# Seven-product projections on one core: accumulators as single PSUM banks, sums on VectorE, x read again for its sums, the attention's loads in a new order

## The chip, the core and the metric

The kernel runs on one core of a Trainium2 chip. The metric is device time in microseconds (us) of one execution. The engines are TensorE (PE in the profile; PEld are its weight loads), VectorE (DVE), ScalarE (ACT), GpSimd (POOL) and SyncE (SP, which here only issues DMAs). Each engine works through its own instructions in order.

## The reference

Two decoder layers, 1024 tokens of width 1024. In each layer one input projection of x feeds three head groups, whose gated outputs are joined, projected and normalized:

```python
for l in range(DEPTH):
    h = x @ w_in[l]
    (hg_q, hg_f, hg_i, hg_gate, mla_cq, mla_ckv, mla_kr, mla_gate,
     mem_q, mem_gate) = jnp.split(h, IN_OFFSETS, axis=-1)
    y_hg = _hgrn2_group(hg_q, hg_f, hg_i, lower_bounds[l], hgrn_out_norm[l])   # 8 heads, gated recurrence
    y_mla = _mla_group(mla_cq, mla_ckv, mla_kr, ...)                           # 8 heads, causal latent attention
    y_mem = _memory_group(mem_q, mem, w_mem_k[l], w_mem_v[l])                  # 4 heads into 256 memory tokens
    y = jnp.concatenate([y_hg * jax.nn.silu(hg_gate), y_mla * jax.nn.silu(mla_gate),
                         y_mem * jax.nn.silu(mem_gate)], axis=-1)
    x = _layernorm(DEEPNORM_ALPHA * x + y @ w_out[l], ln_g[l], ln_b[l])
```

## The kernel before

All large products are float32 made of three fp32r matmuls (`mm3`, lines 252 to 255): both operands are split into a high part (a ScalarE cast, line 238 or 279) and a low remainder (a VectorE subtraction, line 239 or 280). x stands in SBUF transposed as a 2 by 2 grid of blocks, `X[i][j]` (four k chunks i, 512 tokens j), each with a high and a low tile; in the seven-product part they are called B11, B12, B21, B22.

A layer runs in this order: `mem_attn` (memory attention, with its own columns of w_in), `latents_out` (the columns cq, ckv, kr of the attention, and `spread`), `hgrn_group` (everything else of w_in and the recurrence), `mla_prep` and `mla_attend` (the attention), `out_group` (output projection, norm, and `next_x`, which transposes the new x into X for the next layer). A planner, not the program's order alone, puts each engine's instructions in a row: work that comes earlier in the program goes first, and later work fills in where the planner expects an engine to be free. Tiles of a pool wait for each other through semaphores that the framework derives from what each instruction reads and writes.

**Seven products.** `hgrn_group` takes w_in in 18 slabs of 256 columns per layer (`slab_w`, line 665). A slab is a 2 by 2 grid too, and its product with X is made with seven block products in place of eight. Each block product is 12 matmuls of 128x512. It needs sums of weight blocks (S1 to S4, by `diff`, line 676, on GpSimd) and sums of x blocks (T1 to T4, made once per layer by `spread`; T1 overwrites B12). The products go in turn into two halves of one accumulator, `Yb` and `Wb` (line 682), which are the two banks of one PSUM tile `A` of 1024 columns: B11 into Yb, T1 into Wb, T2 on top of Yb, B22 on top of Wb, T3 on top of Yb, B21 into Wb, T4 on top of Yb. Between them partial sums are copied out (`keep`, lines 694 and 696, ScalarE) or added into the result (`put`, line 725 or 728, VectorE). The put of a value slab is followed by PE transposes (line 769), that of a gate slab by a sigmoid (745) and a multiplication on GpSimd (746). The gates of the attention go to DRAM (`MGd`, line 758, SP queue).

**Recurrence.** For each of the 8 heads `levels` makes decays (a tree of products `tots`, line 548, on GpSimd) and a seven-step cascade on VectorE and PE (lines 552 to 570); `hg_out` makes the states and outputs, with a root on GpSimd (line 275) between two VectorE steps (615 and 617); `hg_fin` transposes (625), gates (627) and writes to DRAM (`Yd`, line 629, SP queue). Pools `gr`, `gs`, `h` and `gw` are opened in that order.

**Before and after it.** `latents_out` computes the latents of token half 1 (in A tiles), then calls `spread`, then computes half 0 (in the four B tiles of PSUM) and normalizes it (`norm`, lines 846 to 856); the transposes of `turn` (line 864) need a B tile. `spread` rebuilds x as high plus low (lines 645 and 654, VectorE and GpSimd). `mla_prep` loads the latents `ckT` and `cqT` through GpSimd's queue, then `rtab` and the four gate tiles `mg` through ScalarE's queue, then `w_uv` and `w_uk` through SP; `mla_attend` loads `w_uq` through SP, and `q_proj` and `k_proj` follow.

## Time and profile before

| | |
|---|---|
| median of 3 runs | 2344.51 us (2344.29 to 2348.54) |
| profiled execution | 2345.01 us |
| its span, first to last instruction | 2342.8 us |
| mean granted TensorE clock | 0.977 |
| `hgrn_group`, layer 0 and layer 1 | about 209 to 779 us and 1378 to 1957 us of the span |

The profile is of one execution. Busy times of PE have modelled ends, and a few matmul records can be missing, so waits are read from the rows that name them and from distances between starts. "idle before <- releaser" is the time in which an engine had nothing running before an instruction, and what ended it. A wait for several things is put down to the last one.

### The profile page before, as it was taken

How to read it: one execution, taken by the hardware profiler on the slowest of the kernel's cores; microseconds unless marked ns; L12 is line 12 of the kernel's file. 1: busy time of each engine (PE TensorE's matmuls, PEld its weight loads, DVE VectorE, ACT ScalarE, POOL GpSimd, SP SyncE). 2: the span in 40 equal slices, each digit the busy share in tenths (PEclk: the TensorE clock that was granted, in tenths of full speed). 3: DMA queues.
4: the chain of work that ended last, by engine and by line, in shares of the span. 5: the costliest groups of instructions: out<-in, count | busy, mean ns of one | idle time of the engine just before them, and what ended most of it. 6: DMA issues, size and time to landing. Idle time of an engine off the chain costs nothing. (4 is left out here: it accounts for less than half of the span.)

```text
span 2342.8 us, 30451 instructions
## 1 busy us (share of the span) xinstructions
PE 2112.8 (90%) x11176; PEld 1758.1 (75%) x11176; DVE 1422.5 (61%) x2353; ACT 997.1 (43%) x1987; POOL 710.2 (30%) x784
## 2 busy tenths in 40 slices
PE   9996899898998599999999968989898985999998
PEld 7885677777777488878787856767677774888886
DVE  6456566746566488756854565656465664888424
ACT  5434343434343377634544343334233333777211
POOL 0235232423314255401101452313232232554012
PEclk9998999999999899999999989999999997999999
DMA  6311111111111500266640111111111015003422
GB/s 197 104 41 72 37 37 36 39 52 37 54 36 48 186 13 12 84 215 227 221 145 33 37 72 37 45 35 39 45 37 54 19 63 189 11 13 107 158 83 81
DMA packets 112628, 178.74 MB, mean 76 GB/s; under 512 B 7584, under 2 KB 81184, under 8 KB 112480
## 3 DMA queue, kind: packets, MB, share of 16 engines
q1 hardware_dynamic: 104656, 150.10, 19.4%
q10 hardware_dynamic: 4752, 15.95, 2.0%
q0 software_dynamic: 3072, 10.75, 1.2%
q8 instruction: 88, 1.44, 0.3%
q14 instruction: 60, 0.49, 0.1%
HBM read 140.60 MB, written 36.18 MB: 75 GB/s over the span
## 5 line engine op out<-in xcount | busy, mean ns | idle before, releaser
L253 PE MATMUL A<-x,wh 128*128 128x512 f32 x800 | 332.9, 418 | 43.7 <-ACT pt L694 23.0
L254 PE MATMUL A<-x,wh 128*128 128x512 f32 x800 | 320.1, 400 | 0.0
L255 PE MATMUL A<-x,wl 128*128 128x512 f32 x800 | 318.0, 399 | 0.0
L678 POOL TENSOR_TENSOR S<-raw 128x512 f32<-128x512 f32 x72 | 101.4, 1409 | 489.0 <-DVE wl L280 356.3
L253 PEld LDWEIGHTS A<-x,wh 128*128 128x128 f32 x800 | 153.5, 192 | 92.6 <-ACT pt L694 34.3
L253 PE MATMUL A<-t,wh 128*128 128x512 f32 x432 | 181.3, 420 | 33.4 <-DVE G L725 13.1
L279 ACT CAST wh<-raw 128x512 fp32r<-128x512 f32 (+1 forms) x124 | 72.8, 591 | 291.4 <-PE A L254 150.9
L239 DVE TENSOR_TENSOR wl<-raw,wh 128x512 fp32r<-128x512 f32 (+2 forms) x216 | 142.2, 703 | 88.8 <-ACT wh L238 88.6
L279 ACT CAST wh<-S 128x512 fp32r<-128x512 f32 x144 | 89.3, 620 | 247.6 <-PE A L254 168.4
L255 PEld LDWEIGHTS A<-x,wl 128*128 128x128 f32 x800 | 152.8, 191 | 32.0
L280 DVE TENSOR_TENSOR wl<-S,wh 128x512 fp32r<-128x512 f32 x144 | 123.3, 859 | 84.7 <-ACT wh L279 84.4
L254 PEld LDWEIGHTS A<-x,wh 128*128 128x128 f32 x800 | 153.6, 192 | 27.0 <-DVE x L280 0.6
L255 PE MATMUL A<-t,wl 128*128 128x512 f32 x432 | 171.2, 396 | 0.0
L254 PE MATMUL A<-t,wh 128*128 128x512 f32 x432 | 170.6, 395 | 0.0
L238 ACT CAST wh<-raw 128x512 fp32r<-128x512 f32 (+2 forms) x216 | 118.2, 606 | 100.3 <-PE A L254 43.6
L1009 POOL TENSOR_SCALAR pr<-pr,rs 128x512 f32<-128x512 f32 (+1 forms) x192 | 116.8, 617 | 145.1 <-DVE rs L1006 125.6
L561 PEld LDWEIGHTS B<-Q,r 128*128 128x128 f32 x896 | 116.3, 191 | 42.3 <-ACT r L556 22.2
L280 DVE TENSOR_TENSOR wl<-raw,wh 128x512 fp32r<-128x512 f32 (+1 forms) x124 | 83.9, 681 | 103.9 <-ACT wh L279 101.7
L561 PE MATMUL B<-Q,r 128*128 128x128 f32 x896 | 132.7, 292 | 10.7 <-DVE Q L565 8.8
L280 DVE TENSOR_TENSOR pl<-B,ph 128x512 fp32r<-128x512 f32 (+1 forms) x192 | 119.7, 643 | 22.2 <-ACT ph L279 19.1
L253 PEld LDWEIGHTS A<-t,wh 128*128 128x128 f32 x432 | 82.0, 190 | 65.0 <-DVE G L725 17.4
L746 POOL TENSOR_TENSOR G<-G,tmp 128x512 f32<-128x512 f32 x48 | 68.3, 1423 | 182.7 <-ACT tmp L745 182.7
(317 smaller groups left out, 5418.5 us busy)
## 6 DMA issues: line engine op xcount, KB each, us to landing
raw<-in_w_in SPq DMA_DIRECT2D x84, 512.0 KB, 4.5
raw<-in_w_out SPq DMA_DIRECT2D x32, 1024.0 KB, 5.0
yr<-Yd SPq DMA_DIRECT2D x28, 384.0 KB, 4.6
Yd<-r SPq DMA_DIRECT2D x32, 256.0 KB, 2.0
raw<-in_w_mk SPq DMA_DIRECT2D x8, 512.0 KB, 4.4
raw<-in_w_mv SPq DMA_DIRECT2D x8, 512.0 KB, 4.8
Yd<-yt POOLq DMA_DIRECT2D x16, 256.0 KB, 2.4
MGd<-G SPq DMA_DIRECT2D x16, 256.0 KB, 2.0
```

The lines of the kernel that those rows point to most:

```text
L238: nc.scalar.copy(h[:, s_], raw[:, s_])
L239: nc.vector.tensor_tensor(out=lo[:, s_], in0=raw[:, s_], in1=f32(h[:, s_]), op=ALU.subtract)
L253: nc.tensor.matmul(o, lhsT=lh, rhs=rh, start=first, stop=False, **kw)
L254: nc.tensor.matmul(o, lhsT=lh, rhs=rl, start=False, stop=False, **kw)
L255: nc.tensor.matmul(o, lhsT=ll, rhs=rh, start=False, stop=last, **kw)
L279: nc.scalar.copy(h, src)
L280: nc.vector.tensor_tensor(out=lo, in0=src, in1=f32(h), op=ALU.subtract)
L561: nc.tensor.matmul(lp[:, pr * P:(pr + 1) * P], lhsT=xp[:, pr * P:(pr + 1) * P], rhs=q_moving(Q, pr, b), start=True, stop=True)
L678: nc.gpsimd.tensor_tensor(out=t, in0=a, in1=b, op=op)
L746: nc.gpsimd.tensor_tensor(out=g, in0=g, in1=t, op=ALU.mult)
L1009: nc.gpsimd.tensor_scalar(out=pr[:, c0:c1], in0=pr[:, c0:c1], scalar1=rs, scalar2=0.0, op0=ALU.mult, op1=ALU.add)
```

## The change

- The PSUM pool is opened anew around `hgrn_group`. In it Yb and Wb are two tiles of one bank each (`Y`, four buffers) instead of two halves of one A tile. The pool now has `reuse_waits="tile"`.
- `diff`, the multiplication behind the sigmoid and the decay tree go from GpSimd to VectorE. `S` gets four buffers instead of three, `pt` three instead of four.
- The writes of `Yd` (line 629) and `MGd` (758) go from SP's queue to GpSimd's.
- `spread` comes after all latents. It loads the sixteen 128x512 pieces of x from DRAM (ScalarE's queue; xT in layer 0, a new DRAM tensor XT1 in layer 1) and makes its four sums on VectorE alone; ten piece buffers instead of six.
- `next_x` also copies each transposed piece (ScalarE) and writes it to XT1 (ScalarE's queue).
- In `mla_prep` everything but `rtab` is loaded through SP in the order w_uv and w_uk, ckT, w_uq, cqT; the `mg` loads come after the first `q_proj` in the program. `ckT` and `cqT` move to the left pool; the pools of `hgrn_group` are opened in the order `gr`, `h`, `gs`, `gw`, and `r` and `G` move from `h` to `gs`.

```diff
+            self.c = pool(name, bufs=2, space=PSUM, reuse_waits="tile")
...
-            nc.gpsimd.tensor_tensor(out=nt, in0=v[:, :, 0], in1=v[:, :, 1], op=ALU.mult)
+            nc.vector.tensor_tensor(out=nt, in0=v[:, :, 0], in1=v[:, :, 1], op=ALU.mult)
...
-            nc.sync.dma_start(Y[hd, :, hf * 512:(hf + 1) * 512], yt)
+            nc.gpsimd.dma_start(Y[hd, :, hf * 512:(hf + 1) * 512], yt)
...
-            return T(lp, [P, 512], F32, "t", 6)
+            return T(lp, [P, 512], F32, "t", 10)
+        src = xT if l == 0 else XT1
         for k in range(4):
             raw = {}
...
+            for i, j in ((0, 0), (0, 1), (1, 1), (1, 0)):
+                raw[i, j] = piece()
+                nc.scalar.dma_start(raw[i, j], src[(4 * i + k) * P:(4 * i + k + 1) * P, j * 512:(j + 1) * 512])
+            t1, t2, t3, t4 = raw[0, 1], raw[1, 1], piece(), raw[1, 0]
+            nc.vector.tensor_tensor(out=t3, in0=t2, in1=t1, op=ALU.subtract)
+            nc.vector.tensor_tensor(out=t1, in0=t1, in1=raw[0, 0], op=ALU.subtract)
+            nc.vector.tensor_tensor(out=t2, in0=t2, in1=t1, op=ALU.subtract)
+            nc.vector.tensor_tensor(out=t4, in0=t4, in1=t2, op=ALU.subtract)
+            for o, t in ((B12, t1), (T2, t2), (T3, t3), (T4, t4)):
+                split(o[0][:, k], o[1][:, k], t)
...
-            g1, sp, hp, gw = (gs_.enter_context(pool(f"{n}{l}", bufs=1, reuse_waits="tile")) for n in ("gr", "gs", "h", "gw"))
+            g1, hp, sp, gw = (gs_.enter_context(pool(f"{n}{l}", bufs=1, reuse_waits="tile")) for n in ("gr", "h", "gs", "gw"))
...
-                    t = T(g1, [P, 512], F32, "S", 3).rearrange("p (k c) -> p k c", k=4)
-                    nc.gpsimd.tensor_tensor(out=t, in0=a, in1=b, op=op)
+                    t = T(g1, [P, 512], F32, "S", 4).rearrange("p (k c) -> p k c", k=4)
+                    nc.vector.tensor_tensor(out=t, in0=a, in1=b, op=op)
...
-                acc = psA()
-                Yb, Wb = acc[:, 0:512], acc[:, 512:1024]
+                Yb, Wb = (T(pss.p, [P, 512], F32, "Y", 4)[:, :] for _ in range(2))
...
-                    nc.gpsimd.tensor_tensor(out=g, in0=g, in1=t, op=ALU.mult)
+                    nc.vector.tensor_tensor(out=g, in0=g, in1=t, op=ALU.mult)
...
-                slab_w(O_MG + 256 * i2, silu_put(G, lambda i, j, g: nc.sync.dma_start(
+                slab_w(O_MG + 256 * i2, silu_put(G, lambda i, j, g: nc.gpsimd.dma_start(
...
-            ops = spread(l, X, tp, lp)
...
-            return ops
+            return spread(l, X, tp, lp)
...
+        kv = slab_aps(ld_kv, 1024)
+        for i in range(2):
+            nc.sync.dma_start(f32(ckT[i]), CK[l][i])
+        uq = slab_aps(ld_q)
+        for i in range(2):
+            nc.sync.dma_start(f32(cqT[i]), CQ[l][i].rearrange("r p t -> p r t"))
+        nc.scalar.dma_start(rtab, RT)
...
         q_proj(0)
+        for i in range(4):
+            g = T(lp, [P, S], F32, "mg", 4)
+            nc.scalar.dma_start(g, MG[l][i])
+            gs.append(g)
...
+                    xc_ = T(op_, [P, 512], F32, "xc", 2)
+                    nc.scalar.copy(xc_, pt)
+                    nc.scalar.dma_start(XT1[hf * 512:(hf + 1) * 512, tb * P:(tb + 1) * P].rearrange("(k p) t -> p k t", p=P),
+                                        xc_.rearrange("p (k t) -> p k t", k=4))
```

## Rows read from the trace of the kernel before

**Rows 1.** The page, part 1: each engine's busy us, share of span, instructions.
```profile
PE 2112.8 (90%) x11176; PEld 1758.1 (75%) x11176; DVE 1422.5 (61%) x2353; ACT 997.1 (43%) x1987; POOL 710.2 (30%) x784
```

**Rows 2.** Windows: length, busy (count) of PE, PEld, DVE, ACT, POOL, clock, DMA.
```profile
209.00:779.00 570.00, 511.36 (x2646) 410.34 (x2644) 340.29 (x514) 207.28 (x353) 176.02 (x168) 0.99 0.14 48
1378.00:1957.00 579.00, 513.37 (x2636) 411.63 (x2634) 337.53 (x531) 206.27 (x350) 173.78 (x169) 0.98 0.14 47
779.00:810.00 31.00, 11.75 (x44) 8.20 (x43) 11.32 (x20) 11.81 (x23) 5.12 (x6) 0.72 0.89 320
1957.00:1986.00 29.00, 11.49 (x36) 8.48 (x36) 11.37 (x18) 11.18 (x21) 3.60 (x6) 0.59 0.86 314
```

**Rows 3.** Timeline of PE, 240 to 255 us, layer 0: start, length, [idle before].
```profile
240.03 0.50 PE L253 MATMUL A<-x,wh 128*128 128x512 f32 x1 [1.12 <-ACT pt L694]
...
244.02 0.50 PE L253 MATMUL A<-t,wh 128*128 128x512 f32 x1 [0.97 <-ACT pt L694]
...
251.87 0.50 PE L253 MATMUL A<-t,wh 128*128 128x512 f32 x1 [0.85 <-DVE Q L725]
...
254.72 0.39 PE L253 MATMUL A<-x,wh 128*128 128x512 f32 x1
```

**Rows 4.** PE's waits, whole span, for accumulators: us, times, longest.
```profile
PE A L253 <- ACT pt L694: 27.4, 33, 1.1
...
PE A L253 <- DVE G L725: 21.6, 24, 1.5
PE B L769 <- DVE tmp L725: 17.2, 16, 1.3
...
PE A L253 <- ACT pt L696: 8.7, 9, 1.2
...
PE B L769 <- ACT tmp L721: 0.8, 4, 0.2
```

**Rows 5.** The same view: PE's waits for VectorE within the recurrence.
```profile
PE B L625 <- DVE r L617: 22.7, 13, 3.6
...
PE B L561 <- DVE Q L565: 8.8, 16, 1.2
```

**Rows 6.** Groups by line and shape, VectorE: count, busy us, mean ns, idle before.
```profile
L280 DVE TENSOR_TENSOR wl<-S,wh 128x512 fp32r<-128x512 f32 x144 | 123.3, 859 | 84.7 <-ACT wh L279 84.4
...
L565 DVE TENSOR_TENSOR Q<-Q,tk 128x512 f32<-128x512 f32 x96 | 83.5, 870 | 12.6 <-PE B L561 7.5
...
L565 DVE TENSOR_TENSOR Q<-Q,F 128x512 f32<-128x512 f32 x16 | 11.1, 694 | 9.6 <-PE B L561 9.6
```

**Rows 7.** The same view, GpSimd.
```profile
L678 POOL TENSOR_TENSOR S<-raw 128x512 f32<-128x512 f32 x72 | 101.4, 1409 | 489.0 <-DVE wl L280 356.3 <-DMA raw<-in_w_in 132.7
...
L746 POOL TENSOR_TENSOR G<-G,tmp 128x512 f32<-128x512 f32 x48 | 68.3, 1423 | 182.7 <-ACT tmp L745 182.7
```

**Rows 8.** Timeline, 768 to 832 us: the start of the attention, layer 0.
```profile
790.58 1.06 ACT L279 CAST K<-B 64x512 fp32r<-64x512 f32 x2 [10.01 <-DMA mg<-MGd]
...
795.55 0.80 PE L253 MATMUL B<-ckT,wh 128*128 128x512 f32 x1 [14.92 <-ACT wh L238]
...
801.26 2.18 ACT L238 CAST wh<-raw 128x512 fp32r<-128x512 f32 x4 [5.46 <-DMA raw<-in_w_uq]
```

**Rows 9.** DMA issues: queue, count, KB each, median us from issue to landing.
```profile
raw<-in_w_in SPq DMA_DIRECT2D x84, 512.0 KB, 4.5
raw<-in_w_out SPq DMA_DIRECT2D x32, 1024.0 KB, 5.0
...
raw<-in_w_uq SPq DMA_DIRECT2D x2, 1024.0 KB, 18.0
```

**Rows 10.** Timeline, 190 to 235 us: the end of the latents, layer 0.
```profile
203.62 1.66 POOL L851 TENSOR_TENSOR rst<-ss,mhalf 128x8 f32<-128x8 f32 x1 [3.43 <-DVE ss L848]
...
206.44 3.65 PE L864 MATMUL B<-idr,pr 128*128 128x128 f32 x16 [14.32 <-ACT pr L853]
```

More of the change, by code (lines that the diff above doesn't have):

```diff
@@ L100, in __exit__, with enter, exit @@
             wpc[0].__exit__(None, None, None)
-    ps = es.enter_context(pool("ps", bufs=2, space=PSUM))
+    class _Ps:
+        def enter(self, name):
+            self.c = pool(name, bufs=2, space=PSUM, reuse_waits="tile")
+            self.p = self.c.__enter__()
+        def exit(self):
+            self.c.__exit__(None, None, None)
+    pss = _Ps()
     dr = es.enter_context(pool("dr", bufs=1, space=DRAM))
@@ L636, in piece @@
         def piece():
-            return T(lp, [P, 512], F32, "t", 6)
+            return T(lp, [P, 512], F32, "t", 10)
+        src = xT if l == 0 else XT1
         for k in range(4):
             raw = {}
-            for n, b, e in (("11", B11, nc.vector), ("12", B12, nc.vector), ("22", B22, nc.gpsimd), ("21", B21, nc.gpsimd)):
-                if n == "21":
-                    continue
-                raw[n] = piece()
-                e.tensor_tensor(out=raw[n], in0=f32(b[0][:, k]), in1=f32(b[1][:, k]), op=ALU.add)
-            t3 = piece()
-            nc.gpsimd.tensor_tensor(out=t3, in0=raw["22"], in1=raw["12"], op=ALU.subtract)
-            split(T3[0][:, k], T3[1][:, k], t3)
-            nc.vector.tensor_tensor(out=raw["12"], in0=raw["12"], in1=raw["11"], op=ALU.subtract)
-            nc.gpsimd.tensor_tensor(out=raw["22"], in0=raw["22"], in1=raw["12"], op=ALU.subtract)
-            split(B12[0][:, k], B12[1][:, k], raw["12"])
-            split(T2[0][:, k], T2[1][:, k], raw["22"])
-            r = piece()
-            nc.gpsimd.tensor_tensor(out=r, in0=f32(B21[0][:, k]), in1=f32(B21[1][:, k]), op=ALU.add)
-            nc.gpsimd.tensor_tensor(out=r, in0=r, in1=raw["22"], op=ALU.subtract)
-            split(T4[0][:, k], T4[1][:, k], r)
+            for i, j in ((0, 0), (0, 1), (1, 1), (1, 0)):
[8 more added lines that the diff above has]
+                split(o[0][:, k], o[1][:, k], t)
         return dict(B11=B11, T1=B12, T2=T2, B22=B22, T3=T3, B21=B21, T4=T4)
@@ L751, in gates @@
             def gates(p2):
-                G = [T(hp, [P, S], F32, "G", 2) for _ in range(2)]
+                G = [T(sp, [P, S], F32, "G", 2) for _ in range(2)]
                 slab_w(O_G + 256 * p2, silu_put(G))
@@ L756, in mla_gates @@
             def mla_gates(i2):
-                G = [T(hp, [P, S], F32, "G", 2) for _ in range(2)]
-                slab_w(O_MG + 256 * i2, silu_put(G, lambda i, j, g: nc.sync.dma_start(
+                G = [T(sp, [P, S], F32, "G", 2) for _ in range(2)]
+                slab_w(O_MG + 256 * i2, silu_put(G, lambda i, j, g: nc.gpsimd.dma_start(
                     MG[l][2 * i2 + i, :, j * 512:(j + 1) * 512], g)))
@@ L878, in latents_out @@
                     turn(si, q, c[si])
-            return ops
+            return spread(l, X, tp, lp)
     def mla_prep(l, lp, rp):
-        ckT = [T(rp, [P, S], F32R, f"ckT{i}", 1) for i in range(2)]
-        cqT = [T(rp, [P, 2, S], F32R, f"cqT{i}", 1) for i in range(2)]
+        ckT = [T(lp, [P, S], F32R, f"ckT{i}", 1) for i in range(2)]
+        cqT = [T(lp, [P, 2, S], F32R, f"cqT{i}", 1) for i in range(2)]
         KK = [[T(rp, [P, S], F32R, f"K{ab}{i}", 1) for i in range(2)] for ab in range(2)]
         rtab = T(lp, [P, S], F32, "rtab", 1)
-        for i in range(2):
-            nc.gpsimd.dma_start(ckT[i], CK[l][i])
-        for i in range(2):
-            nc.gpsimd.dma_start(cqT[i], CQ[l][i].rearrange("r p t -> p r t"))
-        nc.scalar.dma_start(rtab, RT)
-        gs = []
-        for i in range(4):
-            g = T(lp, [P, S], F32, "mg", 4)
-            nc.scalar.dma_start(g, MG[l][i])
-            gs.append(g)
         def ld_kv(raw):
@@ L900, in ld_kv, with ld_q @@
             nc.sync.dma_start(raw[:, 512:1024], w_uk[l])
+        def ld_q(raw):
+            nc.sync.dma_start(raw.rearrange("p (r c) -> p r c", r=2), w_uq[l].rearrange("(r p) c -> p r c", p=P))
+        kv = slab_aps(ld_kv, 1024)
[5 more added lines that the diff above has]
+        nc.scalar.dma_start(rtab, RT)
         kb = {}
@@ L942, in mla_prep, with mla_attend @@
         rope_key()
-        kv = slab_aps(ld_kv, 1024)
         k_proj(0)
         k_odd(0)
-        return cqT, ckT, KK, gs, kv, k_proj, k_odd, rtab
-    def mla_attend(l, cqT, ckT, KK, gs, kv, k_proj, k_odd, rtab, lp, rp):
-        def ld_q(raw):
-            nc.sync.dma_start(raw.rearrange("p (r c) -> p r c", r=2), w_uq[l].rearrange("(r p) c -> p r c", p=P))
-        uqh, uql = (t.rearrange("p (r c) -> p r c", r=2) for t in slab_aps(ld_q))
+        return cqT, ckT, KK, uq, kv, k_proj, k_odd, rtab
+    def mla_attend(l, cqT, ckT, KK, uq, kv, k_proj, k_odd, rtab, lp, rp):
+        uqh, uql = (t.rearrange("p (r c) -> p r c", r=2) for t in uq)
+        gs = []
         qt = {}
```

35 lines of the change are left out of this document (21 added, 14 removed).

## The prediction

> **What bounds the kernel now.** I read the busy shares first: TensorE is busy 90% of the span and VectorE 61% [rows 1], so time can only come out of TensorE's gaps, or be lost by making new ones. The windows by stage say where the gaps are [rows 2]. The two stretches of the seven products and the recurrence hold 1149 of the 2342.8 us, at a granted clock of 0.98 to 0.99, so nearly always at the upper level of 2.4 GHz. The two starts of the attention are short and almost empty: 31 and 29 us in which PE is busy 11.75 and 11.49 us, with the DMA engines 0.86 to 0.89 busy and a mean clock of 0.72 and 0.59, a mixture of 2.4 and 1.2 GHz after the engine had stood idle.
>
> Within the long stretches TensorE's timeline shows the pattern [rows 3]. The product that starts at 240.03 goes into Wb and begins a fresh sum there. It still waits, for the copy of Yb (line 694), which is the other bank of the same tile. The next one, into Yb, waits for the copy of Wb. With such a wait a product takes 3.99 us (240.03 to 244.02); without, 2.85 us (251.87 to 254.72). One wait thus costs 1.14 us, a little more than the idle time shown, because the filling and emptying of the array counts as busy. TensorE's wait list has eight such groups behind lines 694, 696, 721, 725 and 728; the four largest and the smallest are shown [rows 4]. The other three are L725 into F (4.3 us, 5 times) and L728 and L725 into Q (4.2 and 3.4, 4 times each). Together: 87.6 us, 99 times. The transposes of the value slabs (line 769) belong to it: the next product is held by the same put, so TensorE has nothing to place before them. Weights are no cause: inside these stretches TensorE's list names no wh or wl.
>
> **Part by part.** The sum is made against the profiled execution, 2345.0 us (span 2342.8 and 2.2 outside); the median of the runs is 0.5 us below that.
>
> *Accumulators as tiles of their own.* A product then waits only for its own bank, which was last used two products earlier. The copy-out (0.6 to 0.7 us, behind at most one cast) has the other bank's product, 2.85 us, to hide in; if that cover were gone the old wait would be back. 99 waits of 1.14 us: **-113 us**. Below, the value cannot be under 0; above, missing matmul records may hide some ten waits more, -125 us.
>
> *Sums on VectorE.* What moves: 4 diffs for each of 36 slabs = 144, 48 gate multiplications [rows 7], and 7 tree steps for each of 16 heads, of 512 elements down to 8. A VectorE operation of two SBUF tiles of 128x512 takes 694 ns where GpSimd is quiet, and 859 to 870 ns on the mean of those that meet GpSimd's sums [rows 6]. New work: 192 x 0.694 = 133 us, and the tree. A tree costs at least one and at most seven full steps, 0.7 to 4.9 us; I take 2.2, since sizes halve: 35 us. Given back, since GpSimd's sums are gone: 144 x (0.859 - 0.694) + 96 x (0.870 - 0.694) = 41 us. Net +127 us on VectorE, which is busy 340.3 + 337.5 = 678 us in the two stretches [rows 2]. After the accumulators' gain these last about 1036 us, so VectorE would be 805 of 1036, 78%. It is in order, and it is in the chain of the weights (diff, cast, remainder) and in the cascade at once, so some of this reaches TensorE. Bounds: all of it, +127 us; at the other end a gain, since TensorE's own waits for VectorE in the recurrence [rows 5], 31.5 us, arise beside GpSimd's sums and could go. I take **+15 us**, nearer to the hidden end, because weights are prepared up to four products ahead (four wh and wl buffers) and 230 us of VectorE stay free.
> Queued behind a diff on VectorE is now everything: a diff that waits for its weight load would hold the cascade. On GpSimd the first diff waited 132.7 us in all for raw [rows 7], at no cost. That is the rival that ends on the other side.
>
> *Start of the attention.* The gates' loads held ScalarE 10 us, since they wait for gates still being written, and the key cast stood behind them [rows 8]. TensorE got its first key product after 14.92 us and then waited for w_uq, whose 1 MB took 18.0 us where another 1 MB load takes 5.0 [rows 9]: some 7 MB were issued at once. In the change the small loads come first in one queue, SP no longer waits on gate and output writes, GpSimd no longer does sums ahead of the ckT and cqT loads, and the pools are laid so that the first of them can start before the stage ends. Idle now: 31 - 11.75 + 29 - 11.49 = 36.8 us; the 23 us of busy time at a mean clock of 0.72 and 0.59 would take some 15 us at full clock, 8 less: 45 us at stake. What is late next is the last load that must wait for space: cqT lies partly on tiles that the final gates use, and one load of 1 MB takes 5.0 us, with 0.6 for a cast, so 5 to 7 us per layer stay. **-31 us**, bounds -10 and -45.
>
> *Latents.* TensorE stands 14.32 us in layer 0 before the transposes [rows 10] and as long in layer 1, because the norm of token half 0, which must free a B tile, queues behind spread on VectorE and ScalarE. With spread last, the norm's own chain stays: eight squares, the 1.66 us root, the scaling, about 6 us. 2 x 8.3 = 16.6. A wait at the first T1 may come in both layers, as T1 now needs 4 MB of x read again, behind ten buffers; at 1 MB per 5.0 us that is 20 us, and the matmuls of both latents run meanwhile, so I take off only 1.6 for it. **-15 us**, bounds +10 and -28.6.
>
> *Copies of x for layer 1.* 16 PSUM copies of about 0.55 us (four casts in 2.18 us [rows 8]) and 16 issues on ScalarE, which is mostly idle there; only the last four lie near the start of layer 1: **+2 us**, bounds 0 and +10. The writes moved to GpSimd's queue have no reader for tens of microseconds. But there a write that waits for its tile stands ahead of the next root (line 275), behind which line 617 on VectorE and the transposes of line 625 on TensorE wait [rows 5]. Were it one product's time in each of 16 heads, 16 x 2.85 = 46 us; as the next root belongs to the head after, whose cascade has just begun, I take 0. SP's queue, freed of these waits, can issue each weight load as its buffer comes free.
>
> Sum: -113 + 15 - 31 - 15 + 2 = -142; 2345.0 - 142 = 2203.
>
> **The rivals.** *VectorE becomes the bound.* The whole +127 us reaches TensorE: 2203 + 112 = 2315; half of it, 64 us, 2203 + 49 = 2252. For it speaks that VectorE runs nearly without a break in each cascade; against, that it has 40% of the stage idle now.
> *VectorE waits for weight loads (the slower side).* There is one raw buffer per slab. Its load is issued when the last weight split of the slab before is done, and takes 4.5 us [rows 9]. With products at 2.85 us, four products, 11.4 us, lie between that split and the next slab's first product, and the cascade may delay the split. If the planner takes loads to be quicker than they are, VectorE stands at each of the 36 first diffs. If it stood the whole load, 36 x 4.5 = 162 us: 2365, slower by 0.9%. It decides the sign once TensorE loses more than 3.9 us per slab by it (142 / 36).
> *The loads move nothing.* The planner may bring the gates' loads forward again, as it does with whatever is ready. Then the same 7 MB stand in front: 2203 + 31 = 2234.
> The Trainium skill says so outright (DMA: Bandwidth & Descriptors, Issuing engines are not separate DMA queues): DMAs of all issuing engines run on the same 16 engines and interleave. The 18.0 us of w_uq beside 5.0 for the same size agree, and by that rule only order and an earlier start can help, not the choice of queue.
> *Everything goes at once.* All accumulator waits, the recurrence's waits, the clock's loss: 2345 - 125 - 31 - 45 - 15 = 2129.
> *The bank is not the cause.* If the wait were for something else that both copies share, the accumulators' term is 0: 2203 + 113 = 2316. The fresh start at 240.03 speaks against it.
>
> **How the numbers follow.** A difference under 0.2% (5 us) can't be told from none. Forecast, 2165 to 2235: 0.58, with the loads' rival (0.10 of it) inside. All at once, below 2165: 0.12. VectorE in part or whole, 2235 to 2315: 0.18. Bank not the cause: 0.03. Within 0.2%: 0.03. Slower by weight loads: 0.06. The range leaves out some 0.05 below 2145 and 0.12 above 2290, which takes in half and more of VectorE's bound and most of the ends of the three smaller terms. Faster 0.91, same 0.03, slower 0.06.
>
> **What would show it.** Right: lines 694, 696 and 725 gone from TensorE's waits, products 2.85 us apart, VectorE's two-input operations all near 694 ns, the windows at the attention's start with a third of the idle time, the 14.3 us before line 864 under 7. Wrong: waits of TensorE for wl or wh (VectorE the bound), of VectorE for raw (weight loads), of ScalarE for mg (loads moved forward).

## The result

| | before | after |
|---|---|---|
| median | 2345.14 us (2344.29 to 2348.54) | 2184.86 us (2183.84 to 2189.00) |
| profiled execution | 2345.0 us, span 2342.8 | 2189.0 us, span 2187.2 |

The ratio is 0.932, 95% interval [0.930, 0.933]: 160 us faster by the medians, 155.6 us by the two spans. The forecast was 2203 us, so the kernel gained 18 us more than I said. Line numbers shift: 694 is now 701, 725 is 732, 746 is 753, 758 is 765, 864 is 871, 253 to 255 are 263 to 265, 280 is 290, 540 is 551, 561 is 572, 565 is 576, 933 is 940, and the tree's line 548 is 559.

The page of the kernel after, part 1, in the form of [rows 1]: busy us, share of the span, instructions.

```profile
PE 2072.6 (95%) x11176; PEld 1761.2 (81%) x11176; DVE 1464.6 (67%) x2665; ACT 1012.3 (46%) x2003; POOL 353.5 (16%) x480
```

TensorE went from 90% to 95% of the span, GpSimd lost half of its work, and VectorE grew by 42 us only, although 166 us of sums moved to it: other operations on it became faster or fell away. The windows of the same stages as in [rows 2]: the seven products of both layers, then both starts of the attention.

```profile
208.00:711.00 503.00, 489.74 (x2632) 409.43 (x2632) 369.47 (x657) 209.43 (x357) 28.72 (x39) 0.99 0.17 55
1301.00:1807.00 506.00, 491.81 (x2632) 411.07 (x2632) 377.78 (x677) 210.90 (x355) 32.32 (x38) 0.98 0.17 54
711.00:735.00 24.00, 10.83 (x41) 8.27 (x41) 10.59 (x21) 10.26 (x17) 3.28 (x5) 0.72 0.81 315
1807.00:1831.00 24.00, 10.45 (x40) 7.88 (x39) 10.59 (x21) 9.99 (x17) 3.21 (x6) 0.72 0.83 315
```

The long stretches fell from 570 and 579 us to 503 and 506; in the short ones TensorE is still idle for more than half of the time. Measured on TensorE's instructions, the gain of 155.6 us divides like this. As the first of the scores counts their first bias product (line 1004, before 999), which starts up to 1.6 us behind the first product of queries and keys.

| stage, both layers together | before | after | difference | forecast |
|---|---|---|---|---|
| last latent product to first slab product | 35.2 | 29.2 | -6.0 | -15 |
| first to last slab product | 1147.6 | 1008.9 | -138.7 | -113 + 15 |
| last slab product to first scores | 60.2 | 48.1 | -12.1 | -31 |
| attention | 349.0 | 344.5 | -4.6 | 0 |
| end of the attention in layer 0 to the last transpose of next_x | 215.2 | 219.9 | +4.7 | +2 |
| the rest | | | +1.2 | 0 |

TensorE's timeline of the kernel after, the same stretch as [rows 3]. Fresh and continued sums now follow each other with no idle time in brackets, 2.72 us apart.

```profile
240.92 0.39 PE L263 MATMUL Y<-t,wh 128*128 128x512 f32 x1
...
243.64 0.39 PE L263 MATMUL Y<-x,wh 128*128 128x512 f32 x1
...
246.36 0.39 PE L263 MATMUL Y<-t,wh 128*128 128x512 f32 x1
```

TensorE's waits of the kernel after, the view of [rows 4 and 5]: us, times, longest.

```profile
PE B L944 <- DVE kb L940: 24.4, 2, 12.2
PE Y L263 <- DVE G L732: 15.3, 4, 5.3
PE B L871 <- ACT pr L860: 10.9, 2, 5.8
PE Y L263 <- ACT wh L289: 9.2, 2, 4.7
PE B L572 <- DVE Q L551: 6.7, 12, 1.2
```

All waits for copies of partial sums are gone, and so are the 22.7 us behind line 617. The waits for w_uq and the key cast [rows 8] are gone too, but a wait of 12.2 us per layer for the rope of the key (line 940) stands in their place. The latents' wait [rows 10] shrank from 14.3 to 5.8 and 5.1 us, and a wait of 4.7 and 4.6 us for the first weights of the products is new. The 15.3 us behind line 732 are products held by a sum into a gate tile, and that sum waits for an earlier gate to land in DRAM (10.5 us, the last row of the next view).

VectorE's groups by line and shape, as in [rows 6], of the kernel after: count, busy us, mean ns, idle before.

```profile
L290 DVE TENSOR_TENSOR wl<-S,wh 128x512 fp32r<-128x512 f32 x144 | 97.9, 686 | 27.3 <-ACT wh L289 26.8
...
L576 DVE TENSOR_TENSOR Q<-Q,tk 128x512 f32<-128x512 f32 x96 | 66.3, 691 | 11.1 <-PE B L572 6.3
L575 DVE TENSOR_TENSOR K<-K,tk 128x512 f32<-128x512 f32 x96 | 65.3, 680 | 0.0
L686 DVE TENSOR_TENSOR S<-raw 128x512 f32<-128x512 f32 x72 | 49.2, 684 | 0.0
...
L732 DVE TENSOR_TENSOR G<-Y,pt 128x512 f32<-128x512 f32 x36 | 24.7, 687 | 28.8 <-PE Y L265 18.0 <-DMA MGd<-G 10.5
```

The remainders wl<-S fell from 859 to 686 ns, the cascade's Q<-Q,tk from 870 to 691.

### The profile page after: what moved, and what is told of

Same layout as the page of the kernel before. It is cut to its first block, busy times and chain, and to the rows that moved or that the text cites. A ratio compares the mean times of both kernels' runs of the same rounds, so it can differ in the third digit from the quotient of the medians.

```text
span 2187.2 us, 30297 instructions
## 1 busy us (share of the span) xinstructions
PE 2072.6 (95%) x11176; PEld 1761.2 (81%) x11176; DVE 1464.6 (67%) x2665; ACT 1012.3 (46%) x2003; POOL 353.5 (16%) x480
## 5 line engine op out<-in xcount | busy, mean ns | idle before, releaser
L263 PE MATMUL Y<-x,wh 128*128 128x512 f32 x576 | 236.7, 411 | 19.8 <-DVE G L732 10.6
L265 PE MATMUL Y<-x,wl 128*128 128x512 f32 x576 | 235.4, 409 | 1.4 <-DVE wl L290 1.4
L264 PE MATMUL Y<-x,wh 128*128 128x512 f32 x576 | 230.7, 401 | 0.0
L263 PE MATMUL Y<-t,wh 128*128 128x512 f32 x432 | 171.2, 396 | 4.8 <-DVE G L732 4.8
L264 PE MATMUL Y<-t,wh 128*128 128x512 f32 x432 | 171.6, 397 | 0.0
L265 PE MATMUL Y<-t,wl 128*128 128x512 f32 x432 | 169.6, 393 | 0.0
L263 PEld LDWEIGHTS Y<-x,wh 128*128 128x128 f32 x576 | 111.2, 193 | 40.3 <-DVE G L732 11.4
L290 DVE TENSOR_TENSOR pl<-B,ph 128x512 fp32r<-128x512 f32 (+1 forms) x192 | 119.7, 643 | 22.2 <-ACT ph L289 19.3
L265 PEld LDWEIGHTS Y<-x,wl 128*128 128x128 f32 x576 | 110.6, 192 | 23.5 <-DVE wl L290 2.8
L264 PEld LDWEIGHTS Y<-x,wh 128*128 128x128 f32 x576 | 111.0, 193 | 20.0
L1010 ACT ACTIVATE pr<-A,nm 128x128 f32<-128x128 f32 (+7 forms) x128 | 95.6, 748 | 58.5 <-DVE nm L1007 48.9
L285 POOL TENSOR_TENSOR rst<-ss,mhalf 128x4 f32<-128x4 f32 x32 | 36.3, 1134 | 514.3 <-DVE ss L283 495.9
L289 ACT CAST ph<-B 128x512 fp32r<-128x512 f32 (+1 forms) x192 | 102.7, 553 | 31.1 <-PE B L1024 15.4
L290 DVE TENSOR_TENSOR wl<-S,wh 128x512 fp32r<-128x512 f32 x144 | 97.9, 686 | 27.3 <-ACT wh L289 26.8
```

The lines of the kernel that those rows point to most:

```text
L263: nc.tensor.matmul(o, lhsT=lh, rhs=rh, start=first, stop=False, **kw)
L264: nc.tensor.matmul(o, lhsT=lh, rhs=rl, start=False, stop=False, **kw)
L265: nc.tensor.matmul(o, lhsT=ll, rhs=rh, start=False, stop=last, **kw)
L285: nc.gpsimd.tensor_tensor(out=r[:, 0:k], in0=ss, in1=mhalf[:, 0:k], op=ALU.pow)
L289: nc.scalar.copy(h, src)
L290: nc.vector.tensor_tensor(out=lo, in0=src, in1=f32(h), op=ALU.subtract)
```

## The experiments

All times are medians; "after" is 2184.9 us, before was 2344.5 to 2345.6 us beside these runs.

### Banks and sums apart: three runs

The products gained 139 us where 98 were forecast. Two parts meet there, the banks and the sums, so each was undone alone, and the banks were tried alone.

*One tile again* (kernel after):

```diff
-                Yb, Wb = (T(pss.p, [P, 512], F32, "Y", 4)[:, :] for _ in range(2))
+                acc = T(pss.p, [P, 1024], F32, "Y", 2)
+                Yb, Wb = acc[:, 0:512], acc[:, 512:1024]
```

> The kernel after, with the two accumulators put back as the two halves of one PSUM tile of two banks; the sums stay on VectorE. Theory (as in the prediction: the shared tile makes a product wait 1.14 us about 99 times): slower than the kernel after by about 113 us, so near 2298 us, and TensorE's list shows the waits for the copies and puts again, about a hundred of them. Rival (most of the 139 us that the two long stretches gained come from the sums on VectorE, not from the banks): slower by 60 us or less, under 2245 us. Other end (the banks alone made all 139 us): about 2324 us.

Measured: 2282.0 us, ratio to before 0.973 [0.971, 0.974], so 97 us slower than after. TensorE's waits and two starts of its timeline, this kernel:

```profile
PE Y L263 <- ACT pt L702: 24.0, 25, 1.1
PE B L777 <- DVE tmp L733: 17.9, 16, 2.0
...
PE B L636 <- DVE r L628: 9.8, 5, 2.1
```

```profile
242.10 0.50 PE L263 MATMUL Y<-t,wh 128*128 128x512 f32 x1 [0.97 <-ACT pt L702]
...
246.08 0.50 PE L263 MATMUL Y<-x,wh 128*128 128x512 f32 x1 [0.97 <-ACT pt L702]
```

The waits return with the tile: 71 us in 72 of them. A product is again 3.98 us from the next, against 2.72 without, so one wait costs 1.26 us, not 1.14: the 2.85 us that I had taken for a product without wait held the refilling after an earlier one. With 72 waits that is 91 of the 97 us. The waits of the recurrence's transposes for line 628 (617 before the change) are back too, 9.8 us in 5 places, although GpSimd makes no sums here.

*Sums back on GpSimd* (kernel after; single banks stay):

```diff
-            nc.vector.tensor_tensor(out=nt, in0=v[:, :, 0], in1=v[:, :, 1], op=ALU.mult)
+            nc.gpsimd.tensor_tensor(out=nt, in0=v[:, :, 0], in1=v[:, :, 1], op=ALU.mult)
...
-                    nc.vector.tensor_tensor(out=t, in0=a, in1=b, op=op)
+                    nc.gpsimd.tensor_tensor(out=t, in0=a, in1=b, op=op)
...
-                    nc.vector.tensor_tensor(out=g, in0=g, in1=t, op=ALU.mult)
+                    nc.gpsimd.tensor_tensor(out=g, in0=g, in1=t, op=ALU.mult)
```

> The kernel after, with the weight sums, the gate multiplications and the decay tree back on GpSimd; single banks stay. As the prediction's step had it (sums on VectorE cost 15 us): faster than the kernel after by about 15 us, near 2170 us. Theory now, after reading the trace (VectorE's two-input operations fell from 859 and 870 ns to 686 and 691, and the recurrence's 22.7 us of waits for line 617 are gone): putting them back costs about 25 to 40 us, so 2210 to 2225 us, and the waits behind the root come back. Rival (VectorE has so much room that it makes no difference): 2180 to 2190 us.

Measured: 2219.8 us, ratio to before 0.946 [0.945, 0.948]: 35 us slower than after. The step of the prediction has the wrong sign. VectorE's groups of this kernel, then GpSimd's largest group, then one place on the three engines' timelines (in order of engine: GpSimd, VectorE, TensorE) and TensorE's wait:

```profile
L290 DVE TENSOR_TENSOR wl<-S,wh 128x512 fp32r<-128x512 f32 x144 | 150.7, 1050 | 102.8 <-ACT wh L289 99.3 <-PE Y L265 2.1 <-PE Y L264 0.2
...
L551 DVE TENSOR_TENSOR Q<-Q,F 128x1024 f32<-128x1024 f32 x16 | 27.9, 1745 | 0.0
L732 DVE TENSOR_TENSOR G<-Y,pt 128x512 f32<-128x512 f32 x36 | 24.7, 686 | 19.0 <-PE Y L265 14.9 <-DMA MGd<-G 3.9
```

```profile
L686 POOL TENSOR_TENSOR S<-raw 128x512 f32<-128x512 f32 x72 | 103.2, 1434 | 307.7 <-DMA raw<-in_w_in 207.2 <-DVE wl L290 100.6
```

```profile
305.71 1.72 POOL L686 TENSOR_TENSOR S<-raw,S 128x512 f32<-128x512 f32 x1
...
308.65 2.94 POOL L753 TENSOR_TENSOR G<-G,tmp 128x512 f32<-128x512 f32 x2
...
308.12 1.12 DVE L290 TENSOR_TENSOR wl<-S,wh 128x512 fp32r<-128x512 f32 x1 [1.81 <-ACT wh L289]
...
310.39 2.29 DVE L551 TENSOR_TENSOR Q<-Q,F 128x1024 f32<-128x1024 f32 x1
...
312.82 1.41 PE L572 MATMUL B<-Q,r 128*128 128x128 f32 x5 [3.27 <-DVE Q L551]
```

```profile
PE B L572 <- DVE Q L551: 30.9, 13, 3.6
```

While GpSimd multiplies a gate (308.65 to 311.59), VectorE's Q<-Q,F takes 2.29 us; in the kernel after it takes 1.20 to 1.22 in all sixteen cases. TensorE waits 3.27 us for it, 30.9 us in 13 places against 6.7 in 12 in the kernel after. The two large groups that get slower have both inputs in SBUF: wl<-S goes from 686 to 1050 ns and Q<-Q,F from 1.21 to 1.74 us, while G<-Y,pt, which reads one input from PSUM, stays at 686. Beside what they run decides: of the 144 wl<-S, the 50 with no GpSimd operation beside them took 681 to 694 ns, the 90 beside a weight sum or a gate multiplication 967 to 2923. The eight Q<-Q,F that took 2.28 to 2.29 us all ran beside a gate multiplication, the other eight (1.20 to 1.21 us) beside nothing.
The Trainium skill (SBUF — State Buffer, Who interferes with whom) says the same: a VectorE instruction with two SBUF inputs contends with a GpSimd instruction that reads SBUF, and the order of issue decides which of the two is held. These rows agree.

Slowing is not the whole of the wait, though. Of the 3.27 us, Q<-Q,F is 1.08 us longer than in the kernel after and the remainder at 308.12 is 0.43 us longer; in front of that remainder VectorE stood idle for 1.81 us, waiting for the cast of a sum that GpSimd, behind a gate multiplication, had begun at 305.71 and took 1.72 us for. The same pattern stands at all eight slow places. So the 35 us hold both, operations that are slowed and sums that come late; how they divide, no run here shows.

*The banks alone* (kernel before; the accumulators as above, with the PSUM pool opened anew around `hgrn_group` and `reuse_waits="tile"`):

```diff
-                acc = psA()
-                Yb, Wb = acc[:, 0:512], acc[:, 512:1024]
+                Yb, Wb = (T(pss.p, [P, 512], F32, "Y", 4)[:, :] for _ in range(2))
```

> The kernel before with one part of the change alone: the accumulators as single-bank tiles in a PSUM pool of their own. The prediction's term by itself: 113 us faster than before, near 2232 us. Rival (the banks make all of the 139 us): near 2206 us. Other rival (without the sums on VectorE, weights on GpSimd come too late for products 2.85 us apart, and new waits for wh and wl take a part back): 2255 us or more.

Measured: 2246.0 us, ratio 0.958 [0.956, 0.959]: 99 us faster than before. Its waits name neither weights for the slab products nor copies; the two largest are the attention's loads and the same wait as in the run before:

```profile
PE B L263 <- ACT wh L248: 35.2, 4, 15.4
PE B L571 <- DVE Q L550: 31.8, 15, 3.3
```

The first row is the start of the attention (tile B), as before the change. The 22.7 us behind line 617 [rows 5] are gone here, and in the run with the sums back as well, although GpSimd makes its sums in both: these waits went with the shared tile, and the recurrence's wait for VectorE moved to the first step of each cascade, 31.8 us. The product stretches lost 109 us; 6 of them came back between the latents and the first slab product (41.5 us against 35.2). The three runs together, as the length of the two product stretches:

| | sums on GpSimd | sums on VectorE |
|---|---|---|
| one tile of two banks | 1147.6 (before) | 1107.6 |
| single banks | 1039.0 (banks alone), 1048.0 (after, sums back) | 1008.9 (after) |

Banks give 99 to 109 us, whichever engine has the sums; the sums on VectorE give 30 to 40 us, whichever the tile. To within 10 us they add. The pairs of kernels that differ in one of the two alone are 98.7 us (one tile again), 108.6 (banks alone) and 39.1 (sums back); "before" against "one tile" holds the rest of the change as well.

### Which of the sums: one run

```diff
-            nc.vector.tensor_tensor(out=nt, in0=v[:, :, 0], in1=v[:, :, 1], op=ALU.mult)
+            nc.gpsimd.tensor_tensor(out=nt, in0=v[:, :, 0], in1=v[:, :, 1], op=ALU.mult)
```

> The kernel after with the decay tree alone back on GpSimd; weight sums and gate multiplications stay on VectorE. With all three back (the second run) it was 35 us slower than after. Theory A (what costs is that GpSimd's 128x512 sums slow VectorE's operations beside them: the mean of wl<-S rose from 686 to 1050 ns, of Q<-Q,F from 1.21 to 1.74 us; the tree is the smallest part of these): within 8 us of after, 2185 to 2193 us. Theory B (the tree is a link of the recurrence's chain, and seven steps on GpSimd come too late for the cascade): 15 to 35 us slower than after, 2200 to 2220 us, with new waits of TensorE or VectorE behind the tree.

Measured: 2183.8 us, ratio 0.931 [0.930, 0.933], the same as after. The tree alone is not a link that TensorE waits for; the 35 us hang on the weight sums and gate multiplications, or on the tree queued behind them. The slow Q<-Q,F all stand beside gate multiplications; what the weight sums cost alone, no run here tells.

### The start of the attention: five runs

The start gained 12 us where 31 were forecast. The kernel after, timelines of 704 to 724 us, the DMA queues' own rows among them (in order of engine: GpSimd, VectorE, TensorE), and the landing time of the gate writes (queue, count, KB, median us):

```profile
713.18 0.54 POOL L765 DMA_DIRECT2D MGd<-G  x1 [1.68 <-DVE G L753]
720.64 0.29 DVE L936 TENSOR_TENSOR kb<-kr,cosk 128x128 f32<-128x128 f32 x1 [7.76 <-DMA MGd<-G]
...
723.07 1.94 PE L944 MATMUL B<-idr,kb 128*128 128x128 f32 x8 [12.19 <-DVE kb L940]
```

```profile
MGd<-G POOLq DMA_DIRECT2D x16, 256.0 KB, 7.8
```

SyncE's queue of the same kernel:

```profile
695.08 14.77 SPq L1126 DMA_DIRECT2D raw<-in_w_out  x2
709.90 0.93 SPq L903 DMA_DIRECT2D ckT<-CKd  x2
710.93 4.02 SPq L906 DMA_DIRECT2D cqT<-CQd  x2
```

The rope's tile kb lies on the space of the gate tiles G. The last gate's write, issued at 713.18, must land before VectorE may write kb, and it takes about 7 us (before, on SP's queue, the median was 2.0). I had said that these writes have no reader for tens of microseconds; no reader, but the next owner of their space. Besides, ckT goes out only at 709.90, behind the second of two early w_out loads, which holds the queue.

*The gates' writes on SP's queue again:*

```diff
-                slab_w(O_MG + 256 * i2, silu_put(G, lambda i, j, g: nc.gpsimd.dma_start(
+                slab_w(O_MG + 256 * i2, silu_put(G, lambda i, j, g: nc.sync.dma_start(
```

> The kernel after, with only the writes of the attention's gates (MGd) back on SP's queue. In the trace of after, the rope of the key waits 7.8 us for the last of these writes to land, and TensorE behind it 12.2 us per layer; a gate sum waits 5.2 us for an earlier one. Theory A (the write is slow because the attention's loads are in flight when it is issued; in SP's queue it goes in front of them and lands in about 2 us): the wait of 12.2 us shrinks to about 4 and the 5.2 us go, so 10 to 25 us faster than after, 2160 to 2175 us. Rival B (SP's queue then holds the loads of w_uq, ckT and cqT behind the gates, as before the change, and TensorE waits for those): no gain or up to 18 us slower, 2185 to 2203 us.

Measured: 2189.2 us, ratio 0.934 [0.932, 0.935]: no gain. The gate writes land in 4.3 us (median) instead of 7.8, not in the 2 us of theory A, and the products' wait for the gate sum, which theory A had going, stays at 15.8 us. TensorE's waits, this kernel:

```profile
PE B L944 <- DVE kb L940: 8.9, 2, 4.5
...
PE B L264 <- DMA cqT<-CQd: 7.1, 2, 3.6
...
PE B L263 <- DMA ckT<-CKd: 5.5, 2, 3.4
...
PE B L263 <- DMA cqT<-CQd: 4.8, 2, 2.6
```

The rope's wait fell by 15.5 us in all, and 17.4 us of waits for ckT and cqT, which stood behind it, came forward.
The Trainium skill (DMA: Bandwidth & Descriptors, Issuing engines are not separate DMA queues) has all DMAs run on the same 16 engines, whichever engine issues them. The run agrees in so far as another queue changed which wait is last, not the time.

*Another layout* (pt, tmp and G above the weights' buffers; the rope's scratch a tile of its own):

```diff
-            g1, hp, sp, gw = (... for n in ("gr", "h", "gs", "gw"))
+            g1, hp, rr_, pp, gw = (... for n in ("gr", "h", "gs", "gp", "gw"))
...
-                G = [T(sp, [P, S], F32, "G", 2) for _ in range(2)]
+                G = [T(gw, [P, S], F32, "G", 2) for _ in range(2)]
```

> The kernel after with another layout of SBUF: pt, tmp and G lie higher, so that the key's rope (kb) and the loads of the attention no longer take the space of the gate tiles G. Theory A (the rope waits only because its tile lies on G, whose write to DRAM must land first, and TensorE has everything else): TensorE's 12.2 us before line 944 fall to about 2 in each layer, 2165 us. Theory B (as with the gates on SP's queue, where this wait fell to 4.5 us and waits for ckT and cqT came in its place, since ckT and cqT are issued only at 710 us behind the second w_out load): no gain, 2180 to 2188 us, with waits for ckT and cqT.

Measured: 2183.7 us, ratio 0.931 [0.929, 0.932]: no gain, as theory B had it. The rope's wait is 8.7 us for both layers together, and waits for ckT stand beside it.

*Order of the loads* (w_out and mg in SP's queue behind cqT; layout as in after):

```diff
-            nc.scalar.dma_start(g, MG[l][i])
+            with tc.issue_after(last_in[0]):
+                nc.sync.dma_start(g, MG[l][i])
...
+                    with tc.issue_after(last_in[0]):
+                        if s2 < 2:
+                            early["w", 0, s2] = out_w(l, s2)
```

> The kernel after with the order of loads alone changed: the two early w_out loads and the four mg loads stand in SP's queue behind cqT (in after, the second w_out load holds SP's queue for 14.8 us in front of ckT). The layout is that of after, so the key's rope still takes the space of G. Theory A (the write of the last gate is slow because 7 MB are in flight; with 4 MB of them behind cqT it lands sooner): the wait before line 944 falls from 12.2 us to about 8, 2175 us. Theory B (the write waits as long, whatever is in flight beside it): 2183 to 2188 us. Neither expects the wait to go.

Measured: 2174.4 us, ratio 0.928 [0.926, 0.929]: 10 us faster than after. The gate writes land in 4.9 us instead of 7.8, and the rope's wait is 14.6 us for both layers instead of 24.4. So the write was slow because of what was in flight beside it. Last product to first scores is 7 us shorter (40.9 against 48.1 for both layers); the rest of the 10 us is spread over stretches that scatter by as much.

*Layout and order together, G as four halves:*

```diff
-                G = [T(gw, [P, S], F32, "G", 2) for _ in range(2)]
+                G = [[T(gw, [P, 512], F32, "G", 4) for _ in range(2)] for _ in range(2)]
```

> Layout and order of loads together, and the gate tiles G as four halves of 512 columns instead of two of 1024, so that a gate sum waits for one write less. Theory A (the start of the attention needs kb off G and ckT, cqT ahead of w_out and mg at once; each alone only brings the other's wait forward): last product to first scores falls from 24.1 us to about 12 in each layer, and the gate sum's 5.2 us per layer go: 20 to 34 us faster than after, 2150 to 2165 us. Theory B (the stretch is as long as its 7.5 MB take at 315 GB/s, 24 us, whatever the order): 2178 to 2187 us.

Measured: 2156.0 us, ratio 0.919 [0.917, 0.920]: 29 us faster than after. The time is theory A's, the place is not: last product to first scores is still 22.1 and 22.2 us (after: 24.1 and 24.1), while the product stretches are 26 us shorter, 18 of them idle time of TensorE; the wait for G (15.3 us in after) is gone. The gate halves were not tried alone, so their share is not separated. VectorE and TensorE of this kernel:

```profile
699.04 0.69 DVE L732 TENSOR_TENSOR G<-Y,pt 128x512 f32<-128x512 f32 x1 [4.02 <-DMA MGd<-G]
```

```profile
706.90 1.97 PE L947 MATMUL B<-idr,kb 128*128 128x128 f32 x8 [8.08 <-DVE kb L943]
```

The gate sum on VectorE still waits 4.02 us for a gate write, and the rope is queued behind it. The next run took that wait away as well.

*All mended* (the last head's `hg_fin` ahead of the last gate slab, kb in the space that comes free first, four buffers for ch and cl):

```diff
-                else:
-                    mla_gates(1)
                 hg_fin(l, h0 + 1, o1, G[1], rr_)
+                if p2 == 3:
+                    mla_gates(1)
...
+        k4 = T(lp, [P, NB, P], F32, "kb", 1)
+        rk = T(lp, [P, P], F32, "rk", 1)
         ckT = [T(lp, [P, S], F32R, f"ckT{i}", 1) for i in range(2)]
```

> Layout, order of loads and gate halves as in the run of layout and order, with three things more: the last head's hg_fin stands ahead of the last gate slab in the program, the key's rope has its tile in the space that comes free first, and ch and cl have four buffers. In the run before, the wait before the rope's transposes was still 8.1 us per layer, because VectorE, in order, stood 4.02 us at a gate sum that waited for an MGd write. Theory A (with its tile free early the rope goes ahead of that gate sum): the 8.1 us fall under 2 in each layer, and the latents' 3.5 us per layer come on top: about 20 us faster than layout and order, 2135 to 2145 us. Theory B (TensorE then waits as long for cqT, which now lies on the last outputs of the recurrence): 2145 to 2156 us.

Measured: 2155.5 us, ratio 0.919 [0.918, 0.920]: no faster. VectorE in this kernel:

```profile
704.53 0.69 DVE L753 TENSOR_TENSOR G<-G,tmp 128x512 f32<-128x512 f32 x1
705.13 0.28 DVE L939 TENSOR_TENSOR kb<-kr,cosk 128x128 f32<-128x128 f32 x1
```

VectorE waits for no gate write any more, but the planner still put the rope last, behind the gates and the remainders of w_uq, so TensorE's wait only fell from 8.1 to some 6.4 us per layer. What was won there, 5 us, was lost in the product stretches (493.3 and 495.2 us against 491.1 and 491.6). The four buffers gained nothing here: last latent product to first slab product is 30.3 us for both layers against 29.7 without them. The start of the attention is a stack of late things, and theory A had looked at one.

### The latents: one run

ScalarE of the kernel after, 202 to 208 us:

```profile
202.63 0.69 ACT L874 ACTIVATE ch<-B,sm 128x512 fp32r<-128x512 f32 x1 [1.27 <-DMA CQd<-ch]
203.67 0.69 ACT L874 ACTIVATE ch<-B,sm 128x512 fp32r<-128x512 f32 x1 [0.35 <-DMA CQd<-ch]
206.25 1.36 ACT L874 ACTIVATE ch<-B,sm 128x512 fp32r<-128x512 f32 x2 [1.90 <-DMA CKd<-ch]
207.51 0.61 ACT L289 CAST wh<-raw 128x512 fp32r<-128x512 f32 x1
```

The first weights' cast stands behind scalings of ch that wait for earlier writes of ch to land.

```diff
-                    h, lo = (T(lp, [P, 512], F32R, f"c{x}", 2) for x in "hl")
+                    h, lo = (T(lp, [P, 512], F32R, f"c{x}", 4) for x in "hl")
```

> The kernel after with four buffers instead of two for the split latents (ch and cl in turn). In the trace of after TensorE waits 4.67 and 4.57 us for the first weights of the seven products; on ScalarE these stand behind the last scalings of ch, which wait 1.27, 0.35 and 1.90 us for earlier writes of ch to land. Theory A (these buffers are the new wait that took the place of the 14.3 us): TensorE's wait for the first wh falls by some 3.5 us per layer, 5 to 7 us faster, near 2179 us. Rival B (it is the order, the scalings themselves and the transposes in front, that holds the first weights): within 2 us of after, 2183 to 2187 us.

Measured: 2178.1 us, ratio 0.929 [0.927, 0.931]: 7 us faster than after. ScalarE in this kernel:

```profile
200.52 2.75 ACT L874 ACTIVATE ch<-B,sm 128x512 fp32r<-128x512 f32 x4 [0.17 <-PE B L871]
203.32 0.62 ACT L289 CAST wh<-raw 128x512 fp32r<-128x512 f32 x1
```

The scalings run through, the first weights are cast 4.2 us earlier, and TensorE's wait for them is 1.94 and 2.00 us instead of 4.67 and 4.57. Part of that comes back at once, as a wait for the first remainders (5.6 us against 1.4 in after); last latent product to first slab product is 23.4 us for both layers instead of 29.2.

### The copies of x: one run

```diff
-                nc.scalar.dma_start(raw[i, j], src[(4 * i + k) * P:(4 * i + k + 1) * P, j * 512:(j + 1) * 512])
+                if l == 0:
+                    nc.scalar.dma_start(raw[i, j], xT[(4 * i + k) * P:(4 * i + k + 1) * P, j * 512:(j + 1) * 512])
+                else:
+                    nc.vector.tensor_tensor(out=raw[i, j], in0=f32(X[i][j][0][:, k]), in1=f32(X[i][j][1][:, k]), op=ALU.add)
...
-                    xc_ = T(op_, [P, 512], F32, "xc", 2)
-                    nc.scalar.copy(xc_, pt)
-                    nc.scalar.dma_start(XT1[hf * 512:(hf + 1) * 512, tb * P:(tb + 1) * P].rearrange("(k p) t -> p k t", p=P),
```

> The kernel after without the copy of x for layer 1 (no XT1: no copies from PSUM and no writes in next_x); in layer 1 spread makes its pieces as high plus low, sixteen additions on VectorE, after all latents as in after. The stretch from the end of layer 0's attention to the last transpose of next_x took 215.2 us before and 219.9 after. Theory A (these 4.7 us are the copies): the stretch returns to about 215 us, 2180 us, unless the sixteen additions (11 us of VectorE) come in front of the first T1. Theory B (the stretch differs by the granted clock or by the attention's tail, not by the copies): it stays near 219 to 220 us and the time within 2 us of after. Theory C (the additions delay T1 in layer 1): 5 to 10 us slower than after, 2190 to 2195 us.

Measured: 2178.0 us, ratio 0.929 [0.927, 0.930]: 7 us faster than after. The windows from the end of layer 0's attention to the last transpose, first of the kernel after, then without copies (columns as in [rows 2]):

```profile
907.00:1126.90 219.90, 211.73 (x1033) 175.76 (x1032) 144.59 (x233) 107.15 (x191) 29.28 (x23) 0.99 0.67 225
```

```profile
906.50:1118.10 211.60, 207.70 (x1033) 173.93 (x1032) 143.21 (x231) 99.85 (x178) 26.82 (x23) 1.00 0.65 219
```

The copies cost about 8 us in this stretch, and the sixteen additions in layer 1 cost 1 us or none (last latent product to first slab product: 14.7 us against 13.9). In other runs that kept the copies the stretch was 215.6 to 222.0 us, so single traces scatter by some 6 us; the two that left the copies out gave 211.6 and 211.3. Before, and with the banks alone, where there are no copies either, it was 215.2 and 215.0: it seems that the change gained some 4 us in this stretch by something else, which the copies hide. What that is, no run here shows.

### What adds: one run

```diff
+            T(lp, [P, 64], F32, "pd", 1)
...
-                    h, lo = (T(lp, [P, 512], F32R, f"c{x}", 4) for x in "hl")
+                    h, lo = (T(lp, [P, 512], F32R, f"c{x}", n) for x, n in (("h", 3), ("l", 4)))
```

with the edit of the run before (no copies), on top of "all mended".

> The kernel of the run before this (layout, order of loads, gate halves, hg_fin ahead of the last gate slab, early tile for the rope), with two things changed: the buffers of ch and cl are three and four and lie so that the first weights of the seven products no longer share their space with the last written ones (there the wait for the first wh was still 5.64 and 4.18 us, although four buffers alone had brought it to 1.94 and 2.00), and without the copies of x for layer 1, as in the run without copies. Theory A (these mends are independent of layout and load order, so they add): 6 us for the latents and 7 for the copies, 2155 - 13 = 2142 us. Theory B (they don't add: what layer 1's start saves is lost again at a later wait): 2148 to 2156 us.

Measured: 2150.1 us, ratio 0.917 [0.916, 0.918]: 5 us below the run it stands on and 35 below after; the fastest of these kernels. The copies' gain is there (the stretch is 211.3 us), the latents' gain is not. ScalarE in this kernel:

```profile
205.28 0.69 ACT L877 ACTIVATE ch<-B,sm 128x512 fp32r<-128x512 f32 x1 [2.18 <-DMA CKd<-ch]
```

ScalarE still waits for a write of ch to land, now with three buffers, and TensorE's wait for the first weights is 4.92 and 3.12 us. In "all mended" it was 5.64 and 4.18 with four, there because the first weights' own space was still being written out (their first cast waits 3.80 us for a write of cl). So what the four buffers gave alone did not add to the other mends, and theory B had it.

## Why the prediction came out as it did

The total was 18 us off (14 by the spans), and that is luck in part: by the stage table the product stretches gained 41 us more than forecast, while the start of the attention fell 19 us short, the latents 9 and the copies' stretch 3; the attention, not forecast, gave 5.

**Accumulators, -113 us: right in mechanism, some 15 us too high.** 97 us by the run with one tile, 99 by the run with the banks alone. Two errors nearly cancel: a wait costs 1.26 us, not 1.14, but not all of the 99 counted waits are paid. Some of the time saved turns up at the next wait, as line 571's 31.8 us in the run with the banks alone show, against 8.8 us for line 561 [rows 5].

**Sums on VectorE, +15 us: the step that failed.** It is -35 us. The sizes were right: by the rows the sums are 166 us of new work (I had 133 + 35), the tree 2.1 us (I took 2.2), and VectorE is 73 and 75% busy in the two stretches (I had 78). What I weighed wrongly was the other side. I counted what GpSimd's sums took from VectorE as busy time, 41 us (54 with K<-K,tk, which fell from 810 to 680 ns too), and set it against the new work. But the new work cost TensorE no wait that its list shows, while the slowed operations and the late sums stood in front of the first step of each cascade, for which TensorE waits: 30.9 us with the sums on GpSimd, 6.7 without. I had named a gain of 31.5 us as the lower bound, and then took a value between the bounds, with the four buffers and VectorE's free time as the reason. The size of that bound was nearly right (35 lies just beyond it), its reason only in part: 22.7 of the 31.5 us were waits for the root, and these went with the shared tile, as the run with the banks alone shows. The rows that should have decided were [rows 5 and 6]: TensorE's waits for VectorE, and operations of one shape at 694 and 870 ns.

**Start of the attention, -31 us: right cause, wrong size, and the next late thing missed.** It gave 12. The waits for the key cast and w_uq went, as said. I expected cqT's load to be late next by 5 to 7 us; it was the rope, by 12.2, because its tile inherited the space of G. The runs show that the wait is not alone: with it shortened, ckT and cqT come forward. That w_out's loads hold the queue (14.8 us for the two) was in the code to be seen, since w_out has the same two raw buffers as w_uq.

**Writes moved to GpSimd's queue, 0 us: too low.** I looked for who reads the data and for what is queued behind; the cost is in who takes the space. Moving them back gains nothing by itself, so the term cannot be given a price of its own.

**Latents, -15 us: 6.** The wait before the transposes fell to 5.8 and 5.1 us, as said (about 6). The 1.6 us that I took off for a new wait were 9.2: not the re-read x, but the first weights, behind ch's two buffers. The run with four buffers shows it.

**Copies, +2 us: within the bounds, too low.** About 7 us by the run without them. I had counted only the last four as near the start of layer 1.

**Attention, -4.6 us:** not forecast, and not looked into. It is there in every run but the one with the banks alone (349.4 us), so it belongs to another part of the change.

Of the rivals, none came about: but for the first product of each layer weights are in time (TensorE's waits for wl are 2 us or less), VectorE never stands for raw, and 2184.9 lies inside the main forecast of 2165 to 2235. Two of the signs that I gave for being right did not come: a product is 2.72 us from the next, not 2.85, and TensorE's idle time at the attention's start fell from 36.8 to 26.7 us, not to a third.

## What to carry to other kernels

When work moves off an engine, ask first whose instructions that engine was slowing or keeping waiting, and whether another engine waits for those: equal shapes with different mean times in one view are the sign. A transfer out of SBUF has a cost even without a reader, if the next stage's first tile takes its space: list the next owners of a space, not only the readers of the data. And where several things are late at one place, removing one shows the next; here three edits of one cause each gave nothing, nothing and 10 us, and two together with smaller gate tiles 29.

## What was new about the hardware

- Two halves of one PSUM tile in different banks are waited for together by the semaphores that the framework derives; as two tiles they are not. Nothing in the banks themselves slowed TensorE: in the kernel after, 58 products during which the other accumulator was copied are 2.72 us apart (median), as are 54 without a copy.
- A VectorE operation with two SBUF inputs of 128x512 took 681 to 694 ns where no GpSimd operation ran beside it, and 967 to 2923 beside a sum or multiplication of GpSimd of about 1.43 us (wl<-S, the run with the sums back; mean of all 1050).
- A write of 256 KB landed in 2.0 us (median, before, on SP's queue), in 7.8 us on GpSimd's queue beside the attention's loads, and in 4.9 us on the same queue when 4 MB of these loads were issued later.
